# Attention beside the recurrence's chunks, two branches' gates made early and kept in DRAM

## The chip, the cores and the metric

One core of a Trainium2 chip runs the whole program in one launch. The metric is the device time in microseconds (us), lower is better. TensorE (PE) does the matmuls and transposes, VectorE (DVE), ScalarE (ACT) and GpSimd (POOL) the rest, SyncE (SP) issues the DMAs. Each engine executes its own instructions strictly in the order in which they were put into its list; semaphores make one engine wait for another.

## The reference

Two layers on a sequence of 512 tokens with 1024 channels. Each layer mixes three branches, then an MLP follows:

```
p = h @ w_in                                   # (512, 1024) @ (1024, 7040)
u, q, k, v, zr, gl = split(p)
y_a = multiscale_pool(u)                       # branch 0, pooling
y_b = diff_attention(q, k, v)                  # branch 1, 4 heads x 2 softmaxes, 128 wide values
y_c = rwkv7_bidir(zr)                          # branch 2, a recurrence over 512 steps, both directions
gates  = sigmoid(gl + b_gate)                  # 3 x 1024 columns
merged = sum_n gates[n] * (y[n] @ w_branch[n]) # y[n] 512 wide, 1024 columns out
x = layer_norm(alpha*x + merged @ w_out)
x = layer_norm(alpha*x + relu(x @ w_up)**2 @ w_down)
```

Everything is float32. The recurrence updates a 64x64 state per head: `state = state*w + sa*(kk*a) + v*k`, `y = state @ r`.

## The kernel before, in words

**Matmuls.** A float32 product is three matmuls on split operands (lines 166 to 168, `mm3`): high x high, low x high, high x low. One 128-column slice of a dense product over 1024 channels is 24 matmuls of 128x512, of a product over 512 channels 12. A weight is loaded (`wraw`, SyncE's queue), its high part is a copy on ScalarE (L142), its low part a subtraction (L143) on GpSimd in the mixer and on VectorE in the MLP.

**The recurrence** is done in 8 chunks of 64 steps for both directions together:
- `rw_prep` projects the branch's inputs and forms decays and scaled keys (`rw_direction`); four small products per head and chunk (L603) go to `at`, the matrices of 64 triangular systems.
- `rw_solve` transposes them (L625) and inverts them row by row: a loop of 30 steps on VectorE, two instructions each (L650, L652), and after every fourth step four transposes on TensorE (L639, `out`). Three rounds of small products (`tn`, `first`, `second`, L162) follow.
- `rw_chain` goes through the chunks c0 to c7. Each chunk has three groups of 16 or 32 small products that depend on each other through copies on ScalarE and VectorE, and between them parts of the next chunk that depend only on loads (`rows`, `turned`). `load` brings the next chunk's vectors from DRAM (`ch`, `pb`, `rr`).
- `rw_out` (two halves) normalises, adds the bonus term and gates the output.

**The rest of the mixer:** `pool_branch`; `attention` (per head three projections, then for each 128 queries a softmax pair on PSUM tiles of tag `l` (L971, L972; L975 to L983), a `turn` of four transposes (L990) and after four of them `values`); `gates(n)` and `merge(n)`, 8 slices each; `merge_last` for branch 2, which needs the recurrence.

**What sets the order.** Every stage is a generator that yields its own estimate in us. `weave(main, fill, ratio, start)` runs the main generator and lets the fill produce instructions up to `ratio` times the main one's time; `FILL` holds the ratios. `urgent` gives main instructions priority, `behind` puts fill after the main stage's last matmul. The scheduler then sets each engine's order from priorities and its own estimates; inside `manual_schedule` TensorE keeps the written order. In the kernel before:

| stage | beside it |
|---|---|
| `rw_prep` | pooling, then attention |
| `rw_solve`, loop | `gates(0)`, reading the pooled branch, `merge(0)` |
| `rw_solve`, rest, and chunks c0 to c5 | `merge(1)` (with its gate slices), `gates(2)` |
| chunks c6, c7 | `rw_out(0)` |
| `rw_out(1)` | start of `merge_last` |

PSUM has 8 banks; tags `d` 2, `l` 2, `t` 1, `c` 1, `a` 2 (line 47).

Of the kernel before, what the change touches and what calls it, by code (L numbers as in the profile page):

```python
# [11 lines left out]
F32R = mybir.dt.float32r  # L12
# [6 lines left out]
S = 512  # L19
# [30 lines left out]
FILL = (1.7, 25.0, 2.0, 1.2, 1.2, 6, 0.8)  # L50
# [71 lines left out]
class Enc:  # L122
# [149 lines left out]
    def run(self):  # L272
        tc, nc, a = self.tc, self.nc, self.a
        V, A, G = nc.vector, nc.scalar, nc.gpsimd
        with ExitStack() as ctx:
# [9 lines left out]
            self.yad = self.T(self.dr, [4, 128, S], "yad")  # L285
            self.lo_engine = G
            self.mhalf = self.T(P, [128, 1], "mhalf")
            G.memset(self.mhalf, -0.5)
            with tc.tile_pool(name="LW", bufs=1, side="right") as LW, tc.tile_pool(name="L0", bufs=1, side="right") as L:
# [19 lines left out]
                self.smask = self.T(P, [128, S], "smask")  # L309
                nc.sync.dma_start(self.smask, a["smask"])  # L310
# [69 lines left out]
    def layer(self, l):  # L380
# [6 lines left out]
        with tc.tile_pool(name=f"R{l}", bufs=1) as self.R:  # L387
            rt = ExitStack()
            with ExitStack() as at:
                self.AT = at.enter_context(tc.tile_pool(name=f"AT{l}", bufs=1, side="right"))  # L390
                self.RX = at.enter_context(tc.tile_pool(name=f"X{l}", bufs=1, side="right"))
# [77 lines left out]
    def rw_prep(self):  # L469
# [5 lines left out]
        pss = self.lora_ps  # L475
        if l == 0:
# [228 lines left out]
    def rw_chain(self):  # L705
# [19 lines left out]
        st = self.T(R3, [128, 8, C], "s", 2)  # L725
# [3 lines left out]
        def load(c):  # L729
            chs = []  # L730
            pb = self.T(R3, [128, 2, 8, C], "pb", 2)
            rr = self.T(R3, [128, 8, C], "rr", 2)
            for d in range(2):
                ch = self.first[d] if c == 0 else self.load_products(c, d)
                nc.sync.dma_start(rr[:, d * 4:d * 4 + 4, :], self.sc[c, d, :, :, 3, :])
                for q in range(2):
                    nc.sync.dma_start(pb[halves[q], q, d * 4:d * 4 + 4, :], self.sc[c, d, halves[q], :, 2, :])
                chs.append(ch)
# [4 lines left out]
            return pb, rr, cols  # L743

        def products(pb, cols, suv):


            rq, qk = ([self.T(R3, [128, 8, C], f"{t}{q}", 2) for q in range(2)] for t in ("rq", "qk"))

            def rows(g):  # L750
                pss = [self.acc("a").rearrange("p (a b x) -> p a b x", a=4, b=2) for q in range(2)]
                for i in range(4):
                    pd = g * 4 + i
                    for q, h in enumerate(halves):
                        mm(pss[q][:, i], cols(pd, 1 - q, 2)[h], cols(pd, 3, 2)[h], start=True, stop=True)
                for q in range(2):
# [584 lines left out]
```

## Time and profile before

| | |
|---|---|
| median of 3 runs | 2178.64 us (2176.7 to 2180.63) |
| profiled execution | 2177.25 us, span 2175.4 us |
| TensorE busy | 2070.0 us (95%) |
| VectorE, ScalarE, GpSimd busy | 51%, 39%, 28% |
| mean granted TensorE clock | 0.961 of 2.4 GHz |
| chain that ended last | TensorE 67%, VectorE 14%, DMA 7% |

The two layers run through the same stages, layer 0 from about 43 to 1114 us, layer 1 after that. In layer 0 the last products of `rw_prep` (L603) end at 296, the solve loop runs from 326 to 386, chunk c0 begins at 471, c6 at about 611, `rw_out` ends near 667, `merge_last` at 687. Output projection and MLP follow. The granted clock is 1.0 at 2.4 GHz and 0.5 at 1.2 GHz; a mean between the two says how long each held. Matmul durations in the timeline overlap; the distance of two starts is what one costs.

### The profile page before, as it was taken

The page shows a single profiled execution, that of the slowest core. Times are in us where ns is not written, and L with a number is a line of the kernel's source. Part 1 is how long each engine was busy: PE and PEld are TensorE (multiplying, and loading weights), DVE is VectorE, ACT ScalarE, POOL GpSimd, SP SyncE. Part 2 cuts the span into 40 slices and gives each one's busy share as a digit, 9 for nine tenths or more (in the row PEclk, how much of TensorE's full clock was granted, in tenths as well). Part 3 has the DMA queues.
Part 4 walks back from the last instruction along what each step waited for, and adds up shares of the span by engine and source line. Part 5 has one row for each costly group of instructions (what it writes and reads, how often), then busy time and mean ns, then how long its engine had stood idle before and what let it go on. Part 6 is the DMA issues. An engine that isn't in the chain of part 4 may idle for free.

```text
span 2175.4 us, 32525 instructions
## 1 busy us (share of the span) xinstructions
PE 2070.0 (95%) x13382; PEld 1647.2 (76%) x13382; DVE 1109.1 (51%) x1760; ACT 858.7 (39%) x1341; POOL 611.5 (28%) x407
## 2 busy tenths in 40 slices
PE   6999999999979999999998999999998899999998
PEld 5667776777767888888886776778777688888886
DVE  5878769322246443343266878782222445423423
ACT  5355555324323332232344555562333243322322
POOL 4543353133215400000445433431322163000004
PEclk9999999889979999999999999997999799999999
DMA  6343341145523332332424334411545052323322
GB/s 209 115 131 105 121 156 59 40 110 148 137 72 119 98 93 97 97 97 97 140 93 131 120 97 128 134 59 38 151 130 148 21 176 67 97 97 97 90 95 87
DMA packets 309680, 233.63 MB, mean 107 GB/s; under 512 B 50106, under 2 KB 277880, under 8 KB 309532
## 3 DMA queue, kind: packets, MB, share of 16 engines
q1 hardware_dynamic: 309388, 231.30, 35.6%
q8 instruction: 105, 1.72, 0.3%
q10 hardware_dynamic: 144, 0.26, 0.1%
q14 instruction: 43, 0.35, 0.1%
HBM read 200.05 MB, written 31.47 MB: 106 GB/s over the span
## 4 chain that ended last, share of the span: by engine, by line
PE 67%; DVE 14%; DMA 7%; POOL 4%; ACT 4%; issue 3%; SPq 0%; POOLq 0%; DVEq 0%; ACTq 0%
PE d L166 13%; PE d L168 12%; PE d L167 12%; PE a L162 5%; PE c L162 3%; DMA ch<-sc 3%; PE l L166 2%; PE l L167 2%; PE l L168 2%; DVE x L652 2%; PE t L162 2%; DVE at L650 1%; PE a L166 1%; PE a L167 1%; PE a L168 1%
## 5 line engine op out<-in xcount | busy, mean ns | idle before, releaser
L166 PE MATMUL d<-xh,wh 128*128 128x512 f32 (+1 forms) x1360 | 546.8, 402 | 6.7 <-ACT xh L268 2.4
L168 PE MATMUL d<-xh,wl 128*128 128x512 f32 (+1 forms) x1360 | 538.8, 396 | 0.8 <-POOL wl L143 0.7
L167 PE MATMUL d<-xl,wh 128*128 128x512 f32 (+1 forms) x1360 | 537.4, 395 | 0.0
L143 POOL TENSOR_TENSOR wl<-wraw,wh 128x1024 fp32r<-128x1024 f32 x137 | 337.9, 2468 | 530.1 <-ACT wh L142 507.1
L142 ACT CAST wh<-wraw 128x1024 fp32r<-128x1024 f32 x259 | 271.3, 1048 | 517.8 <-PE d L167 208.0
L143 DVE TENSOR_TENSOR wl<-wraw,wh 128x1024 fp32r<-128x1024 f32 x122 | 160.6, 1317 | 368.2 <-ACT wh L142 368.1
L166 PEld LDWEIGHTS d<-xh,wh 128*128 128x128 f32 x1360 | 258.9, 191 | 78.9 <-issue 14.1
L168 PEld LDWEIGHTS d<-xh,wl 128*128 128x128 f32 x1360 | 258.8, 190 | 67.0 <-issue 7.1
L167 PEld LDWEIGHTS d<-xl,wh 128*128 128x128 f32 x1360 | 259.3, 191 | 57.6 <-issue 3.1
L143 POOL TENSOR_TENSOR wrl<-wraw,wrh 128x1024 fp32r<-128x1024 f32 x16 | 39.2, 2465 | 659.6 <-ACT wrh L142 659.6
L1266 ACT CAST hh<-f 128x512 fp32r<-128x512 f32 x64 | 39.7, 622 | 84.5 <-DVE f L1263 84.5
L1267 DVE TENSOR_TENSOR hl<-f,hh 128x512 fp32r<-128x512 f32 x64 | 44.2, 693 | 41.4 <-ACT hh L1266 41.3
L795 DVE COPY x<-c 128x256 f32<-128x256 f32 x16 | 6.8, 424 | 112.7 <-ACT x L794 112.7
L977 ACT ACTIVATE p<-p,mx 128x512 f32<-128x512 f32 x64 | 46.0, 719 | 43.6 <-DVE mx L976 43.3
L162 PE MATMUL a<-ch 64*128 64x128 f32 x512 | 53.0, 311 | 10.6 <-DMA ch<-sc 10.6
L162 PEld LDWEIGHTS a<-ch 64*128 64x128 f32 x512 | 42.5, 206 | 15.1 <-issue 7.0
L652 DVE TENSOR_TENSOR x<-x,at 128x60 f32<-128x60 f32 (+14 forms) x60 | 51.1, 851 | 1.5
L1263 DVE TENSOR_TENSOR f<-f 128x512 f32<-128x512 f32 x64 | 43.6, 684 | 14.8 <-ACT f L1262 14.8
L758 DVE TENSOR_TENSOR rq<-a,cst 128x256 f32<-128x256 f32 x64 | 27.2, 425 | 44.1 <-PE a L162 31.6
L975 DVE CUSTOM_DVE_ANT_0 p<-l,tb 128x512 f32<-128x512 f32 x64 | 42.5, 683 | 13.8 <-PE t L990 9.6
L168 PE MATMUL l<-wh,hl 128*128 128x512 f32 x112 | 43.6, 389 | 0.0
L167 PE MATMUL d<-wl,hh 128*128 128x512 f32 x112 | 43.6, 389 | 0.0
(531 smaller groups left out, 4039.3 us busy)
## 6 DMA issues: line engine op xcount, KB each, us to landing
wraw<-in_w_in_dram SPq DMA_DIRECT2D x110, 512.0 KB
wraw<-in_w_up_dram SPq DMA_DIRECT2D x64, 512.0 KB
wraw<-in_w_down_dram SPq DMA_DIRECT2D x64, 512.0 KB
sc<-st SPq DMA_DIRECT2D x16, 1280.0 KB
ch<-sc SPq DMA_DIRECT2D x32, 640.0 KB
wraw<-in_w_branch_dram SPq DMA_DIRECT2D x24, 512.0 KB
wraw<-in_w_out_dram SPq DMA_DIRECT2D x16, 512.0 KB
xs<-s SPq DMA_DIRECT2D x16, 256.0 KB
```

What stands on the lines that cost most here:

```text
L142: self.nc.scalar.copy(hi, src)
L143: (eng or self.nc.vector).tensor_tensor(lo, src, hi, ALU.subtract)
L162: self.anchor = self.nc.tensor.matmul(*args, **kw).ins
L166: mm(out, wh, xh, start=first, stop=False)
L167: mm(out, wh, xl, start=False, stop=False)
L168: mm(out, wl, xh, start=False, stop=last)
L652: V.tensor_tensor(ab[:, s + 1:, :, :s], ab[:, s + 1:, :, :s], w, ALU.add)
L975: V.tensor_tensor_reduce(p, ps, bias, op0=ALU.add, op1=ALU.max, scale=1.0, scalar=-3e38, accum_out=mx)
L977: A.activation(p, p, AF.Exp, bias=mx, accum_out=sm[:, m:m + 1])
L1263: V.tensor_tensor(f, f, f, ALU.mult)
L1266: A.copy(hi, f)
L1267: V.tensor_tensor(lo, f, hi, ALU.subtract)
```

## The change

Attention moves from the preparation into the solve and the chunks. In exchange the gates of branches 0 and 1 are computed beside the preparation and the solve, written to a DRAM tensor `gd` slice by slice, and read back by `merge`. `merge(1)` and `gates(2)` move from beside chunks c0 to c5 to beside c6, c7 and both halves of `rw_out`, all of it in written order for TensorE.

| stage | beside it, after |
|---|---|
| `rw_prep` | pooling, `gates(0)` |
| `rw_solve`, loop | `gates(1)`, the first three steps of attention |
| `rw_solve`, rest, and chunks c0 to c5 | the rest of attention, reading the pooled branch, `merge(0)` |
| chunks c6, c7 with `rw_out(0)`, then `rw_out(1)` | `merge(1)`, `gates(2)`, start of `merge_last` |

To make room, `pb`, `rr`, `s` and `qk` have one buffer instead of two, the chunk's load is divided into three (`load`, `load_pb`, `load_rr`), a step (`yield 1.3`) lies between loading a chunk and using it, attention's PSUM tiles of tag `t` become tag `l`, and the pooled branch is split in four pieces of 512 instead of two of 1024.

```diff
-FILL = (1.7, 25.0, 2.0, 1.2, 1.2, 6, 0.8)
+FILL = (0.95, 25.0, 2.0, 1.35, 1.2, 6, 0.8)
...
+            self.gd = self.T(self.dr, [2, NK, 128, S], "gd")
...
-                att = chain(self.pool_branch(), self.attention())
                 with tc.tile_pool(name=f"A{l}", bufs=1) as self.R1:
-                    weave(self.rw_prep(), att, FILL[0], FILL[1])
-                    drain(att)
+                    fill = chain(self.pool_branch(), self.gates(0))
+                    weave(self.rw_prep(), fill, FILL[0], FILL[1])
+                    drain(fill)
...
-                    fill = chain(self.gates(0), self.pool_load(), self.merge(0))
+                    att = self.attention()
+                    fill = chain(self.gates(1), islice(att, 3))
                     steps = self.rw_solve()
                     weave(self.urgent(steps), fill, FILL[2])
                     drain(fill)
-                    fill = chain(self.merge(1), self.gates(2))
-                    for _ in range(int(FILL[5])):
-                        next(fill)
-                    fill = self.behind(fill)
-                    weave(self.urgent(steps), fill, FILL[6])
+                    fill = chain(att, self.pool_load(), self.merge(0))
+                    weave(self.urgent(steps), self.behind(fill), FILL[6])
...
-                with tc.manual_schedule(engines={mybir.EngineType.PE}):
+                with tc.manual_schedule(engines=pe):
                     weave(self.urgent(steps), fill, FILL[3])
-                    fill = alternate(self.rw_out(0), fill)
-                    weave(self.urgent(steps), fill, FILL[4])
                     drain(fill)
-                last = self.merge_last()
-                weave(self.urgent(self.rw_out(1)), self.behind(islice(last, 4)), 1.0)
+                    last = self.merge_last()
+                    fill = chain(self.merge(1), self.gates(2), islice(last, 4))
+                    both = alternate(self.rw_out(0), fill)
+                    weave(self.urgent(steps), both, FILL[4])
+                    drain(self.urgent(alternate(self.rw_out(1), both)))
...
-            ps = self.acc("t")
+            ps = self.acc("l")
...
+            g = self.gc[m] if n == 2 else self.T(self.F, [128, S], "f2", 3)
+            yield from self.gate(n, m, gw, g)
+            if n < 2:
+                self.nc.sync.dma_start(self.gd[n, m], g)
...
-            g = self.mg[m]
-            if n:
-                g = self.T(F, [128, S], "f2", 3)
-                yield from self.gate(n, m, gw, g)
+            g = self.T(F, [128, S], "f2", 3) if n else self.T(F, [128, S], "mg", 8)
+            nc.sync.dma_start(g, self.gd[n, m])
```

The order of TensorE at three places (in the change, attention's lines are 9 higher: L980 and L981 are the logits, L999 is the turn). First the end of the solve loop in layer 0, before: L639 are the loop's transposes, `l` the slices of merge(0), L1009 the end of attention.

```order
L639 MATMUL a_3294<-cst_78,x_587_2804 64x128
L168 MATMUL l_3327<-x_641_3208,wl_3308 128x512
L166 MATMUL l_3327<-x_641_3208,wh_3307 128x512
L1009 MATMUL t_2681<-cst_78,f_558_2679 128x2 x2
L639 MATMUL a_3294<-cst_78,x_587_2804 64x128
L1009 MATMUL t_2681<-cst_78,f_558_2679 128x2 x2
L167 MATMUL l_3327<-x_642_3209,wh_3307 128x512
L639 MATMUL a_3294<-cst_78,x_587_2804 64x128
L168 MATMUL l_3327<-x_641_3208,wl_3308 128x512
L166 MATMUL l_3360<-x_641_3208,wh_3356 128x512
```

The same place after: `d_2501` is attention's last projection of head 0, L967 turns its values, the rows L162 at the end are `tn`.

```order
L168 MATMUL d_2501<-xh_63,wl_2498 128x512
L639 MATMUL a_2188<-cst_79,x_361_1986 64x128
L639 MATMUL a_2239<-cst_79,x_361_1986 64x128 x3
L967 MATMUL l_2528<-cst_79,f_434_2526 128x128 x4
L639 MATMUL a_2239<-cst_79,x_361_1986 64x128
L639 MATMUL a_2324<-cst_79,x_361_1986 64x128 x4
L639 MATMUL a_2387<-cst_79,x_361_1986 64x128 x4
L639 MATMUL a_2484<-cst_79,x_361_1986 64x128 x4
L639 MATMUL a_2543<-cst_79,x_361_1986 64x128 x4
L639 MATMUL a_2560<-cst_79,x_361_1986 64x128 x3
L162 MATMUL a_2570<-cst_79,x_361_1986 32x64
```

Before, merge matmuls lie between the transposes to the loop's end; after, the dense matmuls end with the second of eight groups of four transposes.

Second, a gap of chunk c1 of layer 0, before (c0 to c5 have such gaps throughout): the last matmuls of a dense gate slice (`d_4349`), then the chain's products (`c`, `t`) and the next chunk's `rows` (`a`).

```order
L166 MATMUL d_4349<-xh_63,wh_4352 128x512
L167 MATMUL d_4349<-xl_64,wh_4352 128x512
L168 MATMUL d_4349<-xh_63,wl_4353 128x512
L162 MATMUL c_4435<-x_4406,tt_2793 64x64 x16
L162 MATMUL t_4452<-rr_4095,s_4273 64x64 x16
L162 MATMUL a_4471<-ch_4378 128x128
```

Chunk c3 after, in such a gap: two softmaxes (L980, L981) and two turns (L999) of head 3, the first turn reads the softmax before these, the second the first of these, then the chain's next products.

```order
L980 MATMUL l_4520<-mg_4080,mg_3920 128x512
L981 MATMUL l_4520<-kl_4082,mg_3920 128x512
L980 MATMUL l_4528<-mg_4081,mg_3921 128x512
L981 MATMUL l_4528<-kl_4082,mg_3921 128x512
L999 MATMUL l_4541<-cst_79,p_752_4441 128x128 x4
L980 MATMUL l_4549<-mg_4080,mg_3920 128x512
L981 MATMUL l_4549<-kl_4082,mg_3920 128x512
L980 MATMUL l_4557<-mg_4081,mg_3921 128x512
L981 MATMUL l_4557<-kl_4082,mg_3921 128x512
L999 MATMUL l_4570<-cst_79,p_766_4523 128x128 x4
L162 MATMUL c_4577<-suv_3966,qk_692_4186 64x64
```

Where 12 dense matmuls of a gate or merge slice stood, now stand matmuls whose inputs come from VectorE and ScalarE.

Third, the beginning of chunk c6 of layer 0, before: products of the chain and of `rw_out(0)` (L874 to L898).

```order
L162 MATMUL a_5675<-ch_5636 128x128
L874 MATMUL l_5700<-y_3959,cst_78 128x256 x2
L874 MATMUL l_5706<-y_3959,cst_78 128x256 x2
L884 MATMUL l_5712<-cst_78,f_955_5703 128x2 x4
L884 MATMUL l_5712<-cst_78,f_957_5709 128x2 x4
L898 MATMUL l_5727<-sg_437,g_944_5688 128x256 x2
L898 MATMUL l_5737<-sg_437,g_944_5688 128x256 x2
L162 MATMUL c_5744<-x_5671,tt_2793 64x64 x16
```

And after: the same products, here L883, with a slice of merge(1) (`l_5335`, 12 matmuls) behind them.

```order
L162 MATMUL c_5267<-suv_5087,pb_5096 64x64 x16
L883 MATMUL l_5315<-y_3059,cst_79 128x256 x2
L883 MATMUL l_5321<-y_3059,cst_79 128x256 x2
L166 MATMUL l_5335<-ybh_4701,wh_5331 128x512
L167 MATMUL l_5335<-ybl_4702,wh_5331 128x512
L168 MATMUL l_5335<-ybh_4701,wl_5332 128x512
```

The eight slices of merge(1) are spread over c6, c7 and both halves of `rw_out`; before, no dense matmul lay there.

## Rows read from the trace of the kernel before

**Rows 1.** The page: busy share of the engines; granted clock in 40 slices.
```profile
PE 2070.0 (95%) x13382; PEld 1647.2 (76%) x13382; DVE 1109.1 (51%) x1760; ACT 858.7 (39%) x1341; POOL 611.5 (28%) x407
...
PEclk9999999889979999999999999997999799999999
```
**Rows 2.** Windows: stretch, us, PE, PEld, DVE, ACT, POOL busy, clock, DMA.
```profile
43.00:296.00 253.00, 245.07 (x1197) 177.00 (x1195) 207.28 (x340) 138.66 (x237) 104.78 (x63) 0.99 0.37 112
...
326.00:387.00 61.00, 55.62 (x266) 41.03 (x264) 55.67 (x97) 35.22 (x56) 22.42 (x11) 0.94 0.23 69
...
404.00:472.00 68.00, 67.11 (x722) 54.59 (x721) 13.94 (x23) 14.98 (x22) 19.01 (x15) 0.77 0.24 67
472.00:605.00 133.00, 128.12 (x1610) 104.33 (x1608) 38.17 (x77) 46.10 (x76) 37.73 (x28) 1.00 0.53 138
605.00:672.00 67.00, 49.18 (x553) 42.17 (x550) 29.79 (x62) 15.72 (x32) 7.89 (x5) 0.80 0.16 47
...
1541.00:1675.00 134.00, 130.26 (x1642) 106.00 (x1642) 38.98 (x78) 46.52 (x76) 38.54 (x28) 1.00 0.54 139
1675.00:1738.00 63.00, 48.66 (x510) 41.41 (x506) 26.19 (x55) 13.39 (x26) 7.05 (x5) 0.73 0.17 49
```
**Rows 3.** The solve loop's two lines, 326 to 387: durations min/median/max in ns.
```profile
L652 DVE TENSOR_TENSOR x<-x,at x30: 222/584/2725, 326.9 to 384.9; 128x60 f32<-128x60 f32 x2, 128x116 f32<-128x116 f32 x2, 128x168 f32<-128x168 f32 x2, 128x216 f32<-128x216 f32 x2
...
L650 DVE TENSOR_TENSOR at<-x x30: 221/550/2739, 326.6 to 384.7; 128x60 f32<-128x60 f32 x2, 128x116 f32<-128x116 f32 x2, 128x168 f32<-128x168 f32 x2, 128x216 f32<-128x216 f32 x2
```
**Rows 4.** Timeline of VectorE in the solve loop: start, duration in us.
```profile
350.59 0.64 DVE L650 TENSOR_TENSOR at<-x 128x468 f32<-128x468 f32 x1
351.27 2.73 DVE L652 TENSOR_TENSOR x<-x,at 128x468 f32<-128x468 f32 x1
```
**Rows 5.** Timeline of GpSimd in the solve loop.
```profile
350.58 2.90 POOL L143 TENSOR_TENSOR wl<-wraw,wh 128x1024 fp32r<-128x1024 f32 x1 [4.91 <-ACT wh L142]
```
**Rows 6.** Timeline of TensorE in chunk c4: first, last dense matmul, next step.
```profile
570.12 0.50 PE L166 MATMUL d<-xh,wh 128*128 128x512 f32 x1
...
572.80 0.39 PE L168 MATMUL d<-xh,wl 128*128 128x512 f32 x1
573.12 0.50 PE L162 MATMUL c<-x,tt 64*64 64x64 f32 x9
```
**Rows 7.** Attention's lines, 43 to 387: busy us, mean ns | idle before.
```profile
L977 ACT ACTIVATE p<-p,mx 128x512 f32<-128x512 f32 x32 | 23.0, 719 | 21.6 <-DVE mx L976 21.5
L975 DVE CUSTOM_DVE_ANT_0 p<-l,tb 128x512 f32<-128x512 f32 x32 | 21.3, 683 | 6.7 <-PE t L990 4.9 <-DMA tb<-bs 1.6
...
L983 DVE SCALAR_TENSOR_TENSOR p<-p,rc,p 128x512 f32<-128x512 f32 x16 | 16.0, 999 | 8.0 <-ACT p L982 7.9
L971 PE MATMUL l<-mg,mg 128*128 128x512 f32 x32 | 14.5, 453 | 0.1
L982 ACT ACTIVATE p<-p,rc 128x512 f32<-128x512 f32 x16 | 11.5, 718 | 5.3 <-DVE rc L981 5.2
L993 DVE TENSOR_TENSOR ybl<-t,ybh 128x512 fp32r<-128x512 f32 x16 | 10.9, 682 | 0.1
L990 PE MATMUL t<-cst,p 128*128 128x128 f32 x64 | 10.6, 286 | 0.1
L992 ACT CAST ybh<-t 128x512 fp32r<-128x512 f32 x16 | 9.3, 580 | 7.8 <-PE t L990 7.7
...
L1011 POOL TENSOR_TENSOR ve<-ve,mhalf 128x8 f32<-128x8 f32 x4 | 6.9, 1718 | 9.0 <-DVE ve L1010 9.0
...
L981 DVE TENSOR_TENSOR rc<-rc,lam 128x1 f32<-128x1 f32 x16 | 5.9, 367 | 0.2
```
**Rows 8.** Lines of TensorE, 472 to 605: the next chunk's rows.
```profile
L162 PE MATMUL a<-ch 64*128 64x128 f32 x192 | 15.1, 284 | 4.5 <-DMA ch<-sc 4.5
```
**Rows 9.** Tile tb (attention's bias): idle of its engine until (us, times).
```profile
DMA tb<-bs: 3.7, 2
```
**Rows 10.** Lines of TensorE, 605 to 672: chain steps with idle before them.
```profile
L162 PE MATMUL c<-suv,pb 128*64 128x64 f32 x64 | 4.9, 319 | 1.4 <-ACT suv L772 1.2
...
L162 PE MATMUL a<-cst,ch 64*128 64x64 f32 x64 | 3.9, 253 | 6.2 <-ACT qk L774 6.0
```

More of the change, by code (lines that the diff above doesn't have):

```diff
@@ L729, in load @@
         def load(c):
[L730 to L738, printed above, removed]
+            chs = [self.first[d] if c == 0 else self.load_products(c, d) for d in range(2)]
             def cols(pd, s, n):
@@ L778, in rw_chain, with load_pb, load_rr @@
-        pb, rr, cols = load(0)
-        rq, qk, parts = products(pb, cols, suv)
-        for part in parts:
-            part()
+            return cols
+        def load_pb(c):
+            pb = self.T(R3, [128, 2, 8, C], "pb", 1)
+            for d in range(2):
+                for q in range(2):
+                    nc.sync.dma_start(pb[halves[q], q, d * 4:d * 4 + 4, :], self.sc[c, d, halves[q], :, 2, :])
+            return pb
+        def load_rr(c):
+            rr = self.T(R3, [128, 8, C], "rr", 1)
+            for d in range(2):
+                nc.sync.dma_start(rr[:, d * 4:d * 4 + 4, :], self.sc[c, d, :, :, 3, :])
+            return rr
@@ new lines, in rows @@
+        def rows(pb, cols, rq, g):
+            pss = [self.acc("a").rearrange("p (a b x) -> p a b x", a=4, b=2) for q in range(2)]
+            for i in range(4):
+                pd = g * 4 + i
+                for q, h in enumerate(halves):
+                    mm(pss[q][:, i], cols(pd, 1 - q, 2)[h], cols(pd, 3, 2)[h], start=True, stop=True)
+            for q in range(2):
+                ps, o = pss[q], halves[1 - q]
+                V.tensor_tensor(rq[q][:, g * 4:g * 4 + 4, :], ps[:, :, 1, :],
+                                mk[1].unsqueeze(1).to_broadcast([128, 4, C]), ALU.mult)
+                V.tensor_tensor(pb[o, q, g * 4:g * 4 + 4, :], ps[o, :, 0, :],
+                                mk[0][o].unsqueeze(1).to_broadcast([64, 4, C]), ALU.mult)
@@ new lines, in turned, with keys @@
+        def turned(cols, s):
+            pss = [bank() for q in range(2)]
+            for pd in range(8):
+                for q, h in enumerate(halves):
+                    mm(pss[q][:, pd, :], cols(pd, s[q], 2)[h], i2[h], start=True, stop=True, is_transpose=True)
+            return pss
+        def keys(cols):
+            qk = [self.T(R3, [128, 8, C], f"qk{q}", 1) for q in range(2)]
+            for q, ps in enumerate(turned(cols, (1, 0))):
+                A.copy(qk[q], ps)
+            return qk
@@ L782, in rw_chain, with values, rq_tiles @@
+        def values(cols, suv):
+            for q, ps in enumerate(turned(cols, (4, 5))):
+                o = halves[1 - q]
+                A.copy(suv[o, :, q, :], ps[o])
+        def rq_tiles():
+            return [self.T(R3, [128, 8, C], f"rq{q}", 2) for q in range(2)]
+        cols, pb, rr, rq = load(0), load_pb(0), load_rr(0), rq_tiles()
+        for g in range(2):
+            rows(pb, cols, rq, g)
             yield 1.3
+        qk = keys(cols)
+        yield 1.3
+        values(cols, suv)
@@ L783, in rw_chain @@
+        yield 1.3
         for c in range(NC):
             more = c < NC - 1
-            if more:
-                suvn = suv_tile()
-                pbn, rrn, cols = load(c + 1)
-                rqn, qkn, parts = products(pbn, cols, suvn)
             ps = bank("c")
@@ L796, in rw_chain @@
             if more:
-                parts[0]()
+                suvn, cols, pb, rqn = suv_tile(), load(c + 1), load_pb(c + 1), rq_tiles()
+                yield 1.3
+                rows(pb, cols, rqn, 0)
             yield 2.6
@@ L810, in rw_chain @@
             if more:
-                parts[1]()
+                rr = load_rr(c + 1)
+                rows(pb, cols, rqn, 1)
             yield 2.6
@@ L838, in rw_chain @@
             if more:
-                parts[3]()
+                values(cols, suvn)
                 yield 2.6
-                suv, st, pb, rr, rq, qk = suvn, sn, pbn, rrn, rqn, qkn
+                suv, rq = suvn, rqn
             if c == 5:
@@ L1048, in attention @@
         for h in range(4):
-            ps = self.bcast(rows, h, "t")
+            ps = self.bcast(rows, h, "l")
             V.scalar_tensor_tensor(om[h], om[h], self.pcol(P_SG), ps, ALU.mult, ALU.mult)
@@ L1090, in pool_load @@
     def pool_load(self):
-        yh, yl = (self.T(self.R2, [128, 4, S], "x2", 2, F32R) for _ in range(2))
-        self.ya = [(yh[:, g, :], yl[:, g, :]) for g in range(4)]
+        self.ya = []
         for g in range(0, 4, 2):
@@ L1095, in pool_load @@
             self.nc.sync.dma_start(raw, self.yad[g:g + 2].rearrange("g p t -> p g t"))
-            self.nc.scalar.copy(yh[:, g:g + 2, :], raw)
-            self.nc.gpsimd.tensor_tensor(yl[:, g:g + 2, :], raw, yh[:, g:g + 2, :], ALU.subtract)
+            for i in range(2):
+                self.ya.append(self.split(raw[:, i], [128, S], self.F, ("yah", "yal"), 4, self.nc.gpsimd))
             yield 0.1
```

71 lines of the change are left out of this document (21 added, 50 removed).

## The prediction

> **What bounds the kernel now.** I read the table of busy shares first: TensorE is busy 95% of the span, no other engine above 51% [rows 1]. The line of granted clock under it is below full in a few slices only. The kernel is therefore limited by TensorE, and a change that removes no matmul can only win or lose in the stretches where TensorE idles or runs at the lower of its two levels (1.2 instead of 2.4 GHz). The windows by stage show where [rows 2]. Per layer:
> - preparation of the recurrence (43 to 296): 245.1 of 253 us busy, clock 0.99;
> - the loop on VectorE that solves the triangular systems (326 to 387): 55.6 of 61, clock 0.94, and VectorE busy 55.7;
> - the products that follow it (404 to 472): 67.1 of 68, but clock 0.77;
> - chunks c0 to c5 (472 to 605): 128.1 of 133, clock 1.00;
> - chunks c6, c7 and the recurrence's output (605 to 672): 49.2 of 67, clock 0.80.
>
> The second layer repeats it (1541 to 1738 in the rows). So today the stretch of the last two chunks wastes most, the first six chunks next to nothing. The reason is in the timeline of a chunk [rows 6]: each chain step is followed by 12 dense 128x512 matmuls that wait for nothing, 570.12 to 573.12, 3.0 us or 0.25 us each (0.23 between neighbours). Three microseconds are enough for the copies that the next chain step waits for.
>
> **The change part by part.** No matmul is added or taken away; the sum is over what each stage hides. All figures are per layer, against the profiled execution (2177.25 us; the median of the runs is 1.4 higher).
>
> *Preparation.* Attention leaves, gates 0 and five of gate 1's eight pieces come in. Both are matmuls, so the stage ends earlier by what attention takes with it and every microsecond of that has to be paid later. Its rows show no TensorE idle that attention caused: 0.1 us before the logits' matmuls (L971) and the turn's (L990) [rows 7]. I take 0; at best all 8 idle microseconds of the stage go, at worst 0.
>
> *Solve loop.* Now it has 61 us with a full supply of merge and gate matmuls. How long it is without company: 30 steps of two VectorE instructions, medians 0.584 and 0.550 us [rows 3], 34 us. Today it is stretched by the fill's own VectorE work and by GpSimd: L652 took 2.73 us when a 2.90 us GpSimd split (L143) began in the step before it [rows 4, 5], 2.1 more than its median. After: the order of VectorE has four operations of head 0's projections in the loop (about 0.69 each) and I count three splits, so 34 + 3 x 2.1 + 4 x 0.69 = 43 us. TensorE's order inside it holds one and a bit projections, at 24 matmuls x 0.234 = 5.6 us each, and 32 transposes; the last 25 transposes come with no dense matmul between them. That is some 17 us of work (the two projections 11, transposes 6), so 26 idle, against 5.4 today and 3.7 for the clock (0.06 x 61). Loss 26 - 9 = **17 us**. Bounds: a loop of 34 us gives 8, one as long as today's (58) gives 32. The loop itself being shorter wins nothing: TensorE's work does not shrink, it lands later.
>
> *Products after the loop (404 to 472).* Same work with a little attention behind it, no row speaks for another clock: 0, between -5 and +5.
>
> *Chunks c0 to c5 with attention.* This order is fixed by hand, so TensorE stops wherever the next instruction is not ready. Today's loss is 4.9 us. Attention's pieces are not free of waits as the dense ones are:
> - the last turn of a head stands directly ahead of the values' product, which waits for L992 and L993 (0.58 + 0.68), and the sums of squares stand directly behind it, waiting for a copy and a square of the size of L992 and L982 (0.58 + 0.72) [rows 7]: 2.5 x 4 heads = 10;
> - a softmax takes 2 x 0.683 (L975) + 0.719 (L977) + 0.367 (L981) + 0.718 (L982) + 0.999 (L983) = 4.2 us until its turn can start. Heads 0 to 2 have a projection between; in head 3 only a turn and a softmax lie there (eight matmuls of about 0.2 us, 1.6). Two places x 2.6 = 5;
> - the loads: chunk data already costs 4.5 [rows 8] and bias tables 3.7 for two waits [rows 9]; with short pieces as the only cover I take 10;
> - the last steps of c5 have no piece between them: 5, from the idle that the same steps show in the tail [rows 10];
> - attention's end, GpSimd's power of 1.72 (L1011), then transposes, split, broadcast, product, and merge(0) behind all of it: 7.
>
> Sum 37, less today's 4.9: **loss 32**, of which I take **30**, since some waits overlap. Bounds: if attention waits as little as in the preparation, only the last two remain, 12 - 5 = 7; if each of the 16 softmaxes stalls by 2.6, 42 + 17 - 5 = 54.
>
> *Chunks c6, c7 and the output.* Eight pieces of merge(1) and one of gates(2), 12 to 24 matmuls each, now lie between chain steps that have nothing between them today. Idle there is 67 - 49.2 = 17.8, and a fifth of the 49.2 is lost to the clock: 9.8. Together 27.6. With 9 pieces for some 16 gaps I take a little over half: **gain 15**, bounds 8 and 27.
>
> *Costs at nothing.* The 16 writes and 16 reads of gates in DRAM, 256 KB each, are 8.4 MB a layer; the DMA share in the stages concerned is 0.37 to 0.53 [rows 2]. A read that comes late holds VectorE's product and with it a bank, not the matmul itself; if that cover is gone, 8 reads x 1 us at most. The smaller buffers (one instead of two) add waits on VectorE that run beside matmuls. On SyncE's queue the chunk's loads now stand behind weight loads; that is in the 10 above.
>
> Sum per layer: 0 - 17 - 30 + 15 = -32. Two layers: 64 us slower, 2177.25 + 64 + 1.4 for the median = 2242.
>
> **The rivals.**
> *The tail decides (faster).* Mechanism: in c6 to the output the pieces of merge(1) bring TensorE to the state of [rows 6], 27 us won; in the chunks the attention waits as little as in the preparation (10 lost), because a chain step stands between most softmaxes and their turns; the solve loop falls to 34 us (8 to 10 lost). Net +7 a layer: 2178.6 - 14 = 2164. It decides as soon as chunks and solve together lose less than the tail wins. For it: idle and clock of the tail in both layers, and the 0.1 us at L971 and L990. Against it: that 0.1 was reached in an order that was free to put other matmuls between, this one is not.
> The Trainium skill says in "Perfetto Trace Analysis", section "Optimization Strategy", that interleaving stretches that are limited by different engines may help; here that is attention (VectorE heavy) beside chunks (VectorE 38 of 133 us). By that rule this rival is the likely one. The trace agrees as to the engines' shares, but the chunk stretch has only 4.9 us of idle to win.
>
> *The clock falls in the chunks (slower still).* Small waits all along the chunk stretch bring it to the clock of today's tail: 0.80 with TensorE busy 73% of the time, 0.73 in layer 1 [rows 2]. About 150 us of matmuls at 0.8 cost 30 more a layer: 2242 + 60 = 2302. For it: 0.77 in 404 to 472, where TensorE is busy 99% with small products. Against it: the projections and merge pieces still give every chunk some dense stretch.
> The Trainium skill, "TensorE: Matmul & The Clock Gate", section "A second HAM failure mode: psum-queue depth-cycling", states that a TensorE which idles briefly between groups of matmuls while banks are cycled has its clock go back and forth, and loses throughput by that. Here all of attention goes through two banks. By that rule this rival holds; the trace shows the lower clock in 605 to 672, where such gaps are, and not in 472 to 605.
>
> *Gains and losses cancel:* the tail wins 24, solve and chunks lose 24: 2178. Needs both at the good half of their bounds.
>
> **How the numbers follow.** Forecast 57%, the tail decides 19%, the clock falls 17%, cancel 7%. The forecast's own range is 2195 to 2275 (per layer -8 to -48). With the rivals' edges the range that should hold 8 of 10 is 2162 to 2312. A measurement tells 0.2%, 4.4 us, from no change. Faster: the first rival and a little of the third, 20%; same 6%; slower 74%.
>
> **What would show it.** Right: in the solve loop TensorE busy about 17 of some 43 us; in the chunks TensorE idle at the values' product, the sums of squares, and head 3's turns, 30 us or more in c0 to c5; in c6 to the output idle under 10 us and a clock near 1. The preparation should end about 40 us earlier than 296. Wrong: if the chunks with attention show under 12 us of idle at full clock, or the loop keeps TensorE busy, the rival that is faster holds; if the granted clock of the chunks is 0.8 or lower, the other. My weakest number is the 30.

## The result and the profile after

| | median | range | ratio to before (95% interval) |
|---|---|---|---|
| before | 2179.64 us | 2176.7 to 2182.14 | |
| changed | 2380.47 us | 2375.87 to 2382.81 | 1.0919 [1.0897, 1.0942] |

The change makes the kernel slower by 201 us, three times the forecast of 64. The profiled execution of the changed kernel has a span of 2379.7 us. The page shows the same matmuls with more idle time, and a second thing: where the clock row of [rows 1] dips to 7 in a few slices, it now falls to 6 and 5.

```profile
PE 2165.1 (91%) x13382; PEld 1703.6 (72%) x13382; DVE 1098.2 (46%) x1760; ACT 865.9 (36%) x1345; POOL 613.7 (26%) x411
PEclk9999966777899999999999999578869899999999
```

The windows of the changed kernel, columns as in [rows 2]: preparation, solve loop, the products behind it, chunks c0 to c5, then c6 to the end of the output; and from the solve loop on the same of layer 1.

```profile
43.00:257.00 214.00, 202.68 (x1011) 151.42 (x1010) 160.59 (x209) 96.52 (x146) 97.41 (x60) 0.97 0.45 140
285.00:325.00 40.00, 20.77 (x80) 11.91 (x79) 37.18 (x67) 22.65 (x37) 5.63 (x3) 0.68 0.14 40
325.00:412.00 87.00, 80.29 (x800) 63.87 (x798) 25.12 (x53) 28.38 (x47) 9.19 (x9) 0.66 0.10 27
412.00:662.00 250.00, 205.54 (x1806) 150.83 (x1808) 101.08 (x239) 95.57 (x179) 38.59 (x32) 0.79 0.32 88
662.00:706.00 44.00, 39.14 (x459) 31.78 (x456) 21.43 (x42) 10.16 (x19) 14.34 (x8) 0.97 0.47 128
...
1466.00:1506.00 40.00, 20.64 (x82) 11.79 (x81) 37.09 (x66) 22.67 (x37) 5.48 (x3) 0.68 0.15 40
1506.00:1587.00 81.00, 75.24 (x807) 59.93 (x807) 24.85 (x53) 28.18 (x47) 9.16 (x9) 0.69 0.11 30
1587.00:1830.00 243.00, 200.72 (x1793) 147.08 (x1789) 100.79 (x239) 95.59 (x179) 38.58 (x32) 0.81 0.32 90
1830.00:1876.00 46.00, 42.29 (x459) 34.11 (x460) 20.98 (x41) 9.55 (x17) 14.33 (x8) 0.86 0.44 124
```

A window loses its idle time (length minus busy) and, roughly, its busy time times one minus the granted clock. Read so, layer 0 comes out as follows, in us (the row "products" before is 387 to 472, with the 17 us of 387 to 404 at full clock, shown here):

```profile
387.00:472.00 85.00, 84.11 (x861) 68.36 (x863) 21.36 (x32) 24.64 (x35) 21.37 (x16) 0.82 0.22 60
```

| stage | lost before | lost after: idle + clock | predicted change | measured change |
|---|---|---|---|---|
| preparation | 8 + 2 | 11 + 6 | 0 | -7 |
| solve loop | 5 + 3 | 19 + 7 | -17 | -18 |
| products | 1 + 15 | 7 + 27 | 0 | -18 |
| chunks c0 to c5 | 5 + 0 | 44 + 43 | -30 | -82 |
| c6 to the output | 18 + 10 | 5 + 1 | +15 | +22 |
| sum | 67 | 170 | -32 | -103 |

Twice 103 is 206, and the spans differ by 204. About half of what was added is idle time (49 us a layer), half the clock (54).

In the loop (lines of TensorE, 285 to 325) the idle time stands before the loop's own transposes, as forecast:

```profile
L639 PE MATMUL a<-cst,x 128*64 128x128 f32 x31 | 11.0, 370 | 19.0 <-DVE x L652 19.0
```

In the chunks (lines of TensorE, 412 to 662) it stands before attention's pieces and before the chain's first products of a chunk:

```profile
L162 PE MATMUL a<-ch 64*128 64x128 f32 x192 | 17.6, 325 | 2.9 <-DMA ch<-sc 2.9
L980 PE MATMUL l<-mg,mg 128*128 128x512 f32 x26 | 16.2, 624 | 4.7 <-DVE ybl L1002 3.4 <-DVE mx L984 1.2
...
L999 PE MATMUL l<-cst,p 128*128 128x128 f32 x60 | 13.0, 355 | 7.5 <-DVE mx L984 7.3 <-DVE p L992 0.2
L162 PE MATMUL c<-suv,pb 128*64 128x64 f32 x202 | 11.5, 273 | 5.3 <-ACT suv L781 5.1 <-issue 0.2
L166 PE MATMUL l<-ybh,yal 128*128 128x512 f32 x16 | 9.8, 613 | 7.7 <-ACT ybh L1001 7.7
...
L1018 PE MATMUL l<-cst,f 128*128 128x2 f32 x32 | 4.5, 262 | 5.3 <-ACT f L1014 5.3
...
L967 PE MATMUL l<-cst,f 128*128 128x128 f32 x8 | 1.3, 287 | 2.9 <-ACT f L964 2.9
```

In the last chunk of the six, c5, it stands before the chain's own steps (lines of TensorE, 645 to 662):

```profile
L162 PE MATMUL c<-suv,pb 128*64 128x64 f32 x44 | 2.3, 248 | 0.9 <-ACT suv L781 0.9
...
L162 PE MATMUL a<-cst,ch 64*128 64x64 f32 x32 | 1.7, 230 | 2.5 <-ACT qk L775 2.5
```

Compare L980's mean, 624 ns, with 453 for the same matmul (L971) in [rows 7]: that is the clock. The timeline of TensorE around head 3's softmaxes (start, duration, in brackets the idle time) shows both at once. Up to 553 a logits' matmul lasts 0.5 us. Then TensorE waits 6.2 us for a turn and 1.6 for the values' product, whose matmuls begin at 0.8 us each; the clock comes back near 566. Then it waits 1.3 us for the sums of squares, and the logits behind them last 0.8 us again:

```profile
553.21 0.49 PE L981 MATMUL l<-kl,mg 64*128 64x512 f32 x1
559.88 1.11 PE L999 MATMUL l<-cst,p 128*128 128x128 f32 x4 [6.18 <-DVE mx L984]
562.57 0.80 PE L166 MATMUL l<-ybh,yal 128*128 128x512 f32 x1 [1.58 <-ACT ybh L1001]
...
566.22 0.39 PE L168 MATMUL l<-ybh,yal 128*128 128x512 f32 x1
...
568.64 1.26 PE L1018 MATMUL l<-cst,f 128*128 128x2 f32 x8 [1.34 <-ACT f L1014]
569.76 0.77 PE L980 MATMUL l<-mg,mg 128*128 128x512 f32 x1
```

Not every pause does this: at 580.78 TensorE waited 1.1 us, and the logits at 581.58 still last 0.50 us.

Of the 6.2 us, 3.8 are not VectorE's work: VectorE itself had waited for the bias table of the next head.

```profile
559.12 0.69 DVE L984 CUSTOM_DVE_ANT_0 p<-l,tb 128x512 f32<-128x512 f32 x1 [3.81 <-DMA tb<-bs]
```

### The profile page after: what moved, and what is told of

Read it like the earlier page. It is cut to its first block, busy times and chain, and to the rows that moved or that the text cites. A ratio compares the mean times of both kernels' runs of the same rounds, so it can differ in the third digit from the quotient of the medians.

```text
span 2379.7 us, 32701 instructions
## 1 busy us (share of the span) xinstructions
PE 2165.1 (91%) x13382; PEld 1703.6 (72%) x13382; DVE 1098.2 (46%) x1760; ACT 865.9 (36%) x1345; POOL 613.7 (26%) x411
## 5 line engine op out<-in xcount | busy, mean ns | idle before, releaser
L168 PE MATMUL d<-xh,wl 128*128 128x512 f32 (+1 forms) x1360 | 547.8, 403 | 2.3 <-POOL wl L143 2.3
L167 PE MATMUL d<-xl,wh 128*128 128x512 f32 (+1 forms) x1360 | 545.9, 401 | 0.0
L166 PEld LDWEIGHTS d<-xh,wh 128*128 128x128 f32 x1360 | 265.2, 195 | 91.3 <-issue 17.6
L168 PEld LDWEIGHTS d<-xh,wl 128*128 128x128 f32 x1360 | 264.6, 195 | 69.6 <-issue 4.5
L167 PEld LDWEIGHTS d<-xl,wh 128*128 128x128 f32 x1360 | 265.5, 195 | 59.8 <-issue 0.5
L986 ACT ACTIVATE p<-p,mx 128x512 f32<-128x512 f32 x64 | 45.9, 718 | 104.7 <-DVE mx L985 104.5
L639 PE MATMUL a<-cst,x 128*64 128x128 f32 x64 | 22.7, 369 | 38.1 <-DVE x L652 38.0
L162 PE MATMUL a<-ch 64*128 64x128 f32 x512 | 49.1, 314 | 6.3 <-DMA ch<-sc 5.0
L980 PE MATMUL l<-mg,mg 128*128 128x512 f32 x64 | 40.4, 632 | 12.0 <-DVE ybl L1002 9.4
L644 ACT COPY tt<-a 32x256 f32<-32x256 f32 x64 | 38.0, 593 | 28.8 <-PE a L639 28.3
L162 PEld LDWEIGHTS a<-ch 64*128 64x128 f32 x512 | 39.7, 212 | 12.1 <-issue 8.0
L639 PEld LDWEIGHTS a<-cst,x 128*64 128x64 f32 x64 | 7.8, 123 | 52.0 <-DVE x L652 39.3
L1020 POOL TENSOR_TENSOR ve<-ve,mhalf 128x8 f32<-128x8 f32 x8 | 13.2, 1646 | 122.2 <-DVE ve L1019 122.2
```

Source lines behind the costliest of these rows:

```text
L162: self.anchor = self.nc.tensor.matmul(*args, **kw).ins
L166: mm(out, wh, xh, start=first, stop=False)
L167: mm(out, wh, xl, start=False, stop=False)
L168: mm(out, wl, xh, start=False, stop=last)
L980: mm(ps, q[m][:, qc], k[m], start=True, stop=False)
L986: A.activation(p, p, AF.Exp, bias=mx, accum_out=sm[:, m:m + 1])
```

## The experiments

The theory after the result: short waits of attention in a fixed order cost their own length and, by the pauses, the clock. The rivals: the waits alone; the empty solve loop; the DRAM round trip; the banks. The median of before was 2179.45, 2175.48 and 2180.63 us beside the three groups of runs.

**1. Solve loop kept busy.** `warm(n)` writes n dense 128x512 matmuls into a bank of tag `d`.

```diff
+            if g > 1:
+                self.warm(18)
             ps = self.acc("a")            # in out(g)
```

> The changed kernel with 18 extra dense 128x512 matmuls, whose results nobody reads, before each of the last six groups of transposes in the solve loop. Nothing waits for them but TensorE itself. Clock theory: the changed kernel's loop leaves TensorE half idle (20.8 of 40 us) and the lower clock then lasts into the products behind it (clock 0.64 to 0.66 from 325 to 412); with TensorE busy in the loop these 87 us fall by 12 to 18 per layer, 25 to 35 us in all. Waiting theory (the stretch is long because its products wait for copies): no change, or up to 10 us slower, since the extra matmuls delay the transposes.

Measured 2384.4 us, 4 more than the change. Loop, then products:

```profile
292.00:336.00 44.00, 37.54 (x174) 28.30 (x173) 41.70 (x65) 26.20 (x41) 10.06 (x4) 0.98 0.19 55
336.00:418.00 82.00, 75.62 (x829) 60.44 (x829) 24.78 (x53) 28.01 (x47) 9.15 (x9) 0.69 0.12 33
```

The loop has its clock back (0.98 for 0.68), the products behind it do not (0.69 for 0.66). The low clock there is not inherited from the loop, and idle time filled with useless work wins nothing.

**2. Solve loop filled with the change's own work.**

```diff
-                    fill = chain(self.gates(1), islice(att, 3))
+                    fill = self.behind(chain(self.gates(1), islice(att, 3)))
```

(and `self.anchor` set at L603, L625 and L639, so that "behind" means behind those.)

> The changed kernel with gates(1) and the first attention steps held behind the last transposes issued, so that they lie in the solve loop and not before it. If the empty loop costs what the trace shows there (19 idle us per layer) and nothing else, 15 to 20 us per layer are won: 2340 to 2350. If it also sets the clock of the following 87 us, 30 to 35 per layer: 2310 to 2320. If the preparation loses its cover by it, at most 10 per layer are left: 2360 or more.

Measured 2366.9, 13.6 less than the change. Preparation, loop, products:

```profile
43.00:250.00 207.00, 174.68 (x891) 129.31 (x891) 156.70 (x214) 89.07 (x137) 86.95 (x55) 0.93 0.43 132
270.00:314.00 44.00, 40.04 (x184) 29.80 (x183) 42.04 (x58) 27.95 (x40) 15.01 (x6) 1.00 0.37 114
314.00:409.00 95.00, 89.03 (x885) 70.19 (x883) 28.46 (x59) 36.11 (x58) 16.33 (x12) 0.76 0.17 48
```

The loop is full at full clock, but the preparation that gave up these matmuls now idles 32 us instead of 11. That is the third of the outcomes written down: the work is wanted in both places.

**3. Pauses of attention filled.**

```diff
+            self.warm(6)      # before each turn; 8 before values, 6 before the sums of squares
```

> The changed kernel with 6 extra dense matmuls before each turn, 8 before each values product and 6 before each sum of squares in attention, results unread: 152 matmuls a layer, 36 us at full clock. Clock theory: chunks c0 to c5 (412 to 662, clock 0.71 to 0.95) run at half clock because of the small pauses; with the pauses filled the clock rises above 0.9 and the 250 us fall to 215 to 235 in spite of the added work: 30 to 60 us in all. Waiting theory: the extra matmuls only take the place of waits or add to them, 0 to 25 us slower per layer.

Measured 2348.8, 32 less than the change although 36 us of matmuls a layer were added. Chunks c0 to c5, and the lines of the logits and the turn there (L986 and L1006 in this kernel):

```profile
416.00:642.00 226.00, 205.89 (x1942) 155.84 (x1941) 100.44 (x239) 95.51 (x179) 38.60 (x32) 0.95 0.35 98
...
L986 PE MATMUL l<-mg,mg 128*128 128x512 f32 x26 | 12.9, 495 | 3.4 <-DVE ybl L1009 2.6 <-DVE mx L990 0.8
...
L1006 PE MATMUL l<-cst,p 128*128 128x128 f32 x60 | 9.1, 273 | 1.3 <-DVE mx L990 0.8 <-DVE p L998 0.5
```

Clock 0.95 for 0.79, idle 20 for 44, length 226 for 250. The balance fits: 24 us of idle time taken by the added matmuls, some 33 of clock regained (43 down to 206 x 0.05 = 10), 36 added: 21 less, 24 measured (in layer 1, 243 to 228, it is 15). This is the run that shows the clock as a cost of its own, which can be had back. It does not show whether the pauses or the lack of dense matmuls sets it: the added matmuls shorten the one and supply the other.

**4. Half of attention back in the preparation.**

```diff
-                    fill = chain(self.pool_branch(), self.gates(0))
-                    weave(self.rw_prep(), fill, FILL[0], FILL[1])
+                    att = self.attention()
+                    fill = chain(self.pool_branch(), islice(att, 17), self.gates(0))
+                    weave(self.rw_prep(), fill, 1.7, FILL[1])
...
-                    att = self.attention()
-                    fill = chain(self.gates(1), islice(att, 3))
+                    fill = self.gates(1)
```

> The changed kernel with attention's heads 0 and 1 (and head 2's projections) back beside the preparation, heads 2 and 3 beside the chunks. If the loss goes with the number of softmaxes beside the chunks, about half of the chunks' 85 lost us per layer come back, 35 to 45: 2290 to 2310. If it is a fixed cost of the arrangement (merge(0) in c4 and c5, the end of attention, head 3 without projections, the empty loop), at most 15 per layer: 2350 or more.

Measured 2324.9, 55 less: between the two. c0 to c5 fall from 250 to 171 us, but with 39 us still idle and at clock 0.76; their dense matmuls are fewer too:

```profile
459.00:630.00 171.00, 132.46 (x1545) 103.25 (x1543) 67.03 (x147) 55.92 (x106) 20.97 (x24) 0.76 0.39 106
```

**5. Dense matmuls between the products behind the loop.**

```diff
+            self.warm(8)      # after each group of tn, first and second
```

> The changed kernel with 8 extra dense matmuls, results unread, between the groups of small products after the solve loop (11 places a layer, 88 matmuls, 20.6 us at full clock). These 83 to 90 us run at the low clock for 53 to 63 us, and a busy loop ahead of them did not change that (52 us). If the small products themselves draw the clock down and dense work between them holds it up, the added 20 us cost nothing: 2370 to 2385, with under 25 us at the low clock there. If the low clock is set by something else (the attention that lies there), 2420 or more, and the low clock stays.

Measured 2405.4, 25 more for 41 us of added work, between the two. 327 to 436, then the same stretch of layer 1:

```profile
327.00:436.00 109.00, 104.36 (x912) 80.57 (x913) 24.89 (x54) 28.52 (x48) 9.18 (x9) 0.72 0.10 27
...
1520.00:1622.00 102.00, 95.83 (x880) 73.76 (x880) 25.32 (x55) 28.69 (x48) 9.22 (x9) 0.78 0.08 21
```

The mean clock hides the answer, because the added matmuls lengthen the stretch. The time at the lower clock is twice one minus the mean, times the length: 2 x 0.28 x 109 = 61 us, where the change has 2 x 0.34 x 87 = 59; in layer 1 it is 45 for 50. So the first expectation (under 25 us) fell: these dense matmuls left the low clock of the products nearly as it was.

**6. One bias table.** Heads 1 to 3 use head 0's table.

```diff
-            tb = self.T(self.AT, [128, 896], "tb", 1)
...
-            nc.sync.dma_start(tb, src)
+            if h == 0:
+                tb = self.T(self.AT, [128, 896], "tb", 1)
...
+                nc.sync.dma_start(tb, src)
```

> The changed kernel with the bias table loaded for head 0 alone; heads 1 to 3 use head 0's table, so that this load and its wait are left out. In the trace the table of head 3 holds VectorE 3.8 us and the turn behind it 6.2 us. If the single table buffer is a large part of the chunks' idle time, 5 to 6 us for each of three heads and two layers: 2345 to 2355. If a wait saved there is found again at the next instruction (values, softmax), under 10 us: 2370 or more.

Measured 2369.1, 11 less, about as the second expectation. The turn's wait in c0 to c5 falls from 7.5 to 3.4 us and now names its own data; the idle time of the stretch falls from 44 to 36 us, and its clock is 0.82:

```profile
416.00:652.00 236.00, 200.34 (x1801) 146.92 (x1798) 101.11 (x239) 96.03 (x179) 38.69 (x32) 0.82 0.33 88
...
L999 PE MATMUL l<-cst,p 128*128 128x128 f32 x60 | 13.0, 355 | 3.4 <-DVE p L992 2.8 <-DVE mx L984 0.6
```

**7. Attention's move undone, the rest of the change kept.**

```diff
-                    fill = chain(self.pool_branch(), self.gates(0))
-                    weave(self.rw_prep(), fill, FILL[0], FILL[1])
+                    fill = chain(self.pool_branch(), self.attention())
+                    weave(self.rw_prep(), fill, 1.7, FILL[1])
...
-                    att = self.attention()
-                    fill = chain(self.gates(1), islice(att, 3))
+                    fill = self.gates(0)
...
-                    fill = chain(att, self.pool_load(), self.merge(0))
+                    fill = chain(self.pool_load(), self.merge(0), self.gates(1))
```

> The changed kernel with attention back beside the preparation and the rest as in the change: gates(0) in the solve loop, reading the pooled branch, merge(0) and gates(1) beside the chunks, merge(1) and gates(2) beside the last chunks and the output, gates through DRAM. If attention's move is what costs, and the cover of the last chunks wins the 12 to 15 us a layer that the trace of the change shows there, this is faster than the kernel before: 2150 to 2175. If the DRAM round trip, the single buffers or the new order of the chunk's loads cost as well, 2190 or more.

Measured 2264.6, ratio to before 1.040 [1.0381, 1.042]: 116 of the 201 us are attention's move, with the gates that had taken its place. The faster kernel (2150 to 2175) did not come; the second expectation did. Solve loop, the products behind it, c0 to c2, c3 to c5:

```profile
323.00:368.00 45.00, 34.66 (x125) 23.59 (x125) 38.16 (x81) 26.91 (x48) 5.39 (x4) 0.70 0.12 41
...
368.00:461.00 93.00, 92.46 (x901) 75.33 (x899) 25.39 (x36) 29.76 (x43) 26.43 (x18) 0.82 0.32 98
...
463.00:544.00 81.00, 75.65 (x868) 60.58 (x864) 21.09 (x36) 28.02 (x47) 20.17 (x16) 0.98 0.57 164
544.00:597.00 53.00, 39.53 (x674) 35.50 (x675) 18.20 (x41) 13.89 (x27) 0.91 (x6) 0.69 0.46 113
```

Where dense work remains (c0 to c2) the clock is 0.98; where it has run out it is 0.69 to 0.70, with idle time besides. With attention gone from beside them, the products are back at the 0.82 of the kernel before, with under 1 us idle; in time at the lower clock 33 us, where the kernel before has 31 and the change 59.

**8. The tail's cover alone, on the kernel before.**

```diff
-                    weave(self.urgent(steps), fill, FILL[3])
-                    fill = alternate(self.rw_out(0), fill)
-                    weave(self.urgent(steps), fill, FILL[4])
-                    drain(fill)
-                last = self.merge_last()
-                weave(self.urgent(self.rw_out(1)), self.behind(islice(last, 4)), 1.0)
+                    weave(self.urgent(steps), fill, 0.85)
+                    last = self.merge_last()
+                    both = alternate(self.rw_out(0), chain(fill, islice(last, 4)))
+                    weave(self.urgent(steps), both, FILL[4])
+                    drain(self.urgent(alternate(self.rw_out(1), both)))
```

> The kernel before with one part of the change alone: the fill of the chunks is used more slowly (ratio 0.85 for 1.2), so that some 9 slices of gates(2) are left for c6, c7 and both halves of the output, all in written order. No gates in DRAM. By the trace these stretches lose 18 us idle and 13 to the clock a layer before, and 9 and 4 in the change: 12 to 18 a layer won, 2145 to 2160. If the thinner fill of c0 to c5 brings waits or the low clock there, 2170 to 2185.

Measured 2165.8, ratio 0.9952 [0.9935, 0.9969]: half a percent faster than before, between the two expectations. The tail was won (77 us with 72 busy, for 72 with 59, and with more work in it), part of it lost again in c0 to c5, whose clock is 0.95 for 0.99.

**9. The DRAM round trip alone, on the kernel before.**

```diff
-            yield from self.gate(n, m, gw, gs[m])
+            g = gs[m] if n else self.T(self.F, [128, S], "f2", 3)
+            yield from self.gate(n, m, gw, g)
+            if n == 0:
+                self.nc.sync.dma_start(self.gd[m], g)      # gates(0)
...
+            if n == 0:
+                nc.sync.dma_start(g, self.gd[m])           # merge(0)
```

> The kernel before with one part of the change alone: the eight slices of gates(0) go to DRAM and merge(0) reads them back, 2 x 2 MB in each layer. If the DRAM round trip is hidden, as the prediction had it, 2174 to 2184. If the reads hold merge(0) (8 reads of 1 to 2 us in two layers), 2190 to 2210.

Measured 2221.1, ratio 1.0173 [1.0147, 1.0198]: 40 us slower, more than either expectation. No instruction of TensorE waits for a read. But in the order of TensorE the eight slices of merge(0) now stand behind the solve loop, not in it. Loop, then products:

```profile
320.00:371.00 51.00, 40.58 (x161) 29.89 (x162) 41.98 (x74) 30.88 (x50) 12.66 (x7) 0.80 0.23 75
371.00:498.00 127.00, 126.00 (x1054) 102.82 (x1054) 24.85 (x39) 34.54 (x45) 41.09 (x25) 0.84 0.32 95
```

The loop has 10 us idle and clock 0.80 (5 and 0.94 before), the stretch behind it is 127 us for 88. So no wait for a transfer was found, and what the order shows is a cost of position: where the matmuls that depend on the reads are put. The run does not separate this from the other thing that it changes, the tile of the gates (`f2`, three buffers, in place of `mg`, eight).

**10. Attention back, dense work back where it ran out.**

```diff
-                    fill = self.gates(0)
+                    fill = chain(self.gates(0), self.pool_load(), self.merge(0))
...
-                    fill = chain(self.pool_load(), self.merge(0), self.gates(1))
+                    fill = chain(self.gates(1), self.gates(2))       # ratio 0.85; both to DRAM
...
-                    fill = chain(self.merge(1), self.gates(2), islice(last, 4))
+                    fill = chain(self.merge(1), self.gate_load(), islice(last, 4))
```

> The kernel with attention back, and dense work given back to the places that ran thin in it: merge(0) in the solve loop as before, gates(1) and gates(2) beside c0 to c5 (both through DRAM), merge(1) alone beside c6, c7 and the output. If what is left of the loss there (85 us) is thin fill, nearly all comes back: 2150 to 2185. If it is the divided loads and single buffers of the chunks, or the DRAM traffic (now 3 gates), 2210 or more.

(The lines with a minus are those of run 7.) Measured 2216.8, ratio 1.0171 [1.0156, 1.0187], in its time as the second expectation: 48 of the 85 us come back. c0 to c5 run at 0.99 again, with the divided loads and single buffers, so these cost little; the solve loop is as bare as in run 7 (44 us):

```profile
324.00:368.00 44.00, 33.68 (x122) 22.99 (x121) 37.46 (x77) 26.13 (x47) 5.39 (x4) 0.69 0.11 35
...
486.00:621.00 135.00, 129.37 (x1655) 105.04 (x1649) 35.44 (x76) 48.90 (x82) 30.16 (x25) 0.99 0.60 168
```

**11. Run 8 with ratio 1.0**, and the four steps of `merge_last` only after `rw_out(0)`.

> The kernel with the tail's cover alone, ratio 1.0 for 0.85, so that TensorE's order has one half slice of dense work in each gap of c0 to c5 and one in most gaps of c6, c7 and the output. In the run at 0.85 chunk c0 had 5 us idle and 7 us at the low clock, where the slower ratio left a gap bare. If bare gaps are what costs, 4 to 6 us a layer are won on it: 2152 to 2162. If the dense work taken from the tail costs as much, 2162 to 2170.

Measured 2156.9, ratio 0.9904 [0.9882, 0.9926]: 24 us faster than before, the best of all, and as the first expectation; what the later start of `merge_last` adds to it was not separated. c0 to c5, then the rest to the end of `merge_last`; before, the same two were 141 and 72 us at 0.99 and 0.84:

```profile
473.00:609.00 136.00, 127.75 (x1628) 103.93 (x1630) 39.62 (x80) 46.35 (x77) 34.95 (x28) 0.96 0.52 134
609.00:681.00 72.00, 63.15 (x596) 52.89 (x591) 38.75 (x70) 23.68 (x40) 22.24 (x10) 0.93 0.32 113
```

**12. Attention's turns, values and sums on the banks of tag d.**

```diff
-            ps = self.acc("l")      # turn, values, sums of squares
+            ps = self.acc("d")
```

> The changed kernel with attention's turns, values and sums of squares on the two PSUM banks of tag d instead of the two of tag l, on which the softmaxes are too. The waits of the turn name VectorE's reading of the logits (L984), 7.3 us in c0 to c5. If these waits are for banks, and if the pauses they make hold the clock down, 10 to 20 us a layer: 2340 to 2360. If the wait only moves to the turn's own data, under 8 us in all: 2372 or more.

Measured 2371.0, 9 less, about as the second expectation. The turn's wait is 4.0 us for 7.5 and names its own data, the logits' wait (4.7) is gone, the idle time of c0 to c5 falls from 44 to 35 us, and their clock stays at 0.80.

```profile
414.00:651.00 237.00, 201.69 (x1797) 147.86 (x1795) 101.82 (x239) 95.70 (x179) 38.59 (x32) 0.80 0.34 93
...
L999 PE MATMUL d<-cst,p 128*128 128x128 f32 x60 | 13.0, 355 | 4.0 <-DVE p L992 4.0
```

## Why the prediction was wrong

**The direction was right**, and so were the places: the loop, the chunks, the tail.

**The preparation** ended at 257, the forecast 40 us earlier held (296 to 257). It lost 7 more than the 0 taken (3 idle, 4 by the clock), outside its bounds.

**The solve loop** lost what was worked out, 18 for 17, in a loop of 40 us for 43, with 20.8 busy for 17. Its parts were different: 19 us of idle time where the sum had 26, and 7 by the lower clock (0.68), which the sum left out. That they add up to the same is luck.

**The idle time of the chunks** was nearly right as a sum: 44 us for 37, or 39 net of the 5 before, for the 30 taken. Term by term it is less good. Values and sums of squares 13 for 10; the turn 7.5 for 5, of which run 6 puts some 4 on the bias table; the loads of the chunks 2.9, with the bias table in a sum of 10; the last steps of c5 3.4 for 5; attention's end about 4 for 7. Not foreseen: 4.7 before the logits, some 4 before the chain's first products in c0 to c4, which wait for ScalarE's copy (L781), and 2.9 before the values are turned (L967).

**The step that failed is the clock in the chunks.** The sum priced them by idle time alone and "I take 30"; the lower clock stood only in a rival, at 17% and 30 us a layer. Measured are 43 us in layer 0 and 38 in layer 1. The two do not exclude each other, both came at once: 39 of idle time and 43 of clock make the 82 that layer 0 lost there. Run 3 shows that the clock is a cost of its own: with dense matmuls in the pauses it is 0.95. That the pauses alone set it is not shown. The timeline has it fall behind single pauses, but in runs 6 and 12 the idle time fell by some 9 us with no matmul added, and the clock was still 0.82 and 0.80, for 0.79.

**The second failed step:** the products behind the loop at 0, between -5 and +5, because "no row speaks for another clock". They lose 18 in layer 0, 12 by the clock and 6 idle. Run 1 shows that the empty loop is not the cause. In the kernel before dense slices lie beside these products; in the change softmaxes and turns do. Run 7 takes these away and has dense slices there again: 0.82, 33 us at the lower clock and under 1 us idle, about as before. So it is the change of neighbours that costs. Run 5 left the neighbours and added dense matmuls, and the time at the lower clock stayed at about 60 us; what in the neighbours sets it is open.

**"Costs at nothing"** is not shown to have failed for the change. VectorE waits there for gates read back (`DVE f L1155: 13.3, 6`, us and times, both layers), but TensorE waits for that product only 1.7 us in layer 0. Run 9 shows a cost that the prediction did not think of, position, 40 us in the kernel before. That figure is not part of the change's 201 as it stands, where gates(0) is stored long before its use.

**The tail** won 22 in layer 0 and 18 in layer 1 for 15, and runs 8 and 11 show that part of this gain can be had alone.

**The range.** The upper bound of the chunks, "42 + 17 - 5 = 54", keeps only 17 of the 32 us that the other terms of the sum come to; with all of them it is 42 + 32 - 5 = 69, still below 82, because it too has no term for the clock.

**The rivals.** "The tail decides" fell: the tail's half of its mechanism is right, its price of 10 for the chunks was an eighth of the true one. "The clock falls" was right as to the clock of the chunks (0.79 for its 0.80), and 2302 still too low: the clock cost 43 there for 30, the idle time 9 more than taken, and products and preparation lost 18 and 7. Its remark that all of attention goes through two banks is not quite so: the projections use tag `d`. Run 12 spreads the rest over two more banks, and the clock stays.

The split of the 201 us: attention's move, with the gates put in its place, 116 (run 7 against the change). The other 85 stay with the change's distribution of gates and merges, with dense work missing in the loop and in c3 to c5; run 10 gives back 48 of them. How much of the remaining 37 is the round trip's order was not separated.

## What to carry to other kernels

In this kernel a stretch of TensorE with short pauses cost twice: their length (44 us in the chunks) and, about as much again, the clock of the matmuls around them (43). So a term for idle time needs a second one for the clock beside it, and not a rival that excludes it. Filler is worth as much as its independence: here 12 dense matmuls that wait for nothing covered a gap, and softmaxes with waits of their own did not. Before moving work, count the gaps that its old neighbours leave bare; here one half slice in each gap of c0 to c5 and in most gaps of the tail (run 11) is worth 1%, with nothing moved to DRAM.

## What the runs showed of the hardware that was not expected

TensorE held the lower clock while it was busy nearly all the time: 80.3 of 87 us at 0.66 in 325 to 412, 67.1 of 68 at 0.77 in [rows 2], in both cases with 32x32 and 32x64 products. In run 5, 20.6 us of 128x512 matmuls between the products left the time at the lower clock nearly as it was, 61 us for 59 and 45 for 50. With dense slices of gates and merges beside the products instead of attention it was 31 us in the kernel before and 33 in run 7. What sets the clock there stays open.
